# A hybrid diffusion block: the low part of each streamed weight block is subtracted on GpSimd instead of VectorE

## The chip, the cores and the metric

The kernel runs on one core of one Trainium2 chip. The metric is the device time of one execution in microseconds (us), lower is better. Times given here are the median of several executions; the profile is one execution, and its times count from its first instruction.

The core has five engines that run side by side and wait for each other by semaphores: TensorE (PE in the rows; its weight loads are PEld), VectorE (DVE), ScalarE (ACT), GpSimd (POOL) and SyncE (SP), which issues most of the transfers. Each engine takes its own instructions in order. SBUF is the on-chip memory, PSUM the memory that TensorE writes.

## The reference

Two layers. Each normalises and modulates 512 latent and 256 context tokens of width 1024, and projects them by `w_in` to the inputs of four branches and of four gates. The mixing part is the sum over the branches (a Fourier mix, a convolution, grouped attention, differential attention) of gate times projected branch, and one output projection; a gated feed-forward part follows.

```python
px = jnp.split(hx @ w_in[l], SPLIT_IDX, axis=-1)
...
gates = jax.nn.sigmoid(zgate.reshape(b, l, N_BRANCH, D_MODEL))
ys = jnp.stack([y_four, y_conv, y_gqa, y_diff], axis=2)
return jnp.sum(gates * ys, axis=2) @ lp["w_out"]
```

All is float32. The second layer leaves out the context's own output.

## The kernel before, in words

**Products in three.** Activations lie with features on the 128 partitions and tokens along the row. Each float32 operand of a large product is split into a high part, rounded to the matmul type `float32r`, and a low part, the rest; a product is three matmuls: high by high, high by low, low by high (`mm3u`, lines 603 to 605: weight high `wh` with activations high, with activations low, then weight low `wl` with activations high).

**Streamed weight blocks.** A weight block is 512 rows by 128 columns, in SBUF a 128x512 tile of 256 KB. In the mixing part from the key and query projections on, 264 blocks come through the class `Stream`. Each takes three steps: `dma` issues the load of `ws` on SP (line 553), `hi` rounds it to `wh` on ScalarE (line 559), `lo` subtracts `wl = ws - wh` on VectorE (line 566). There are three buffers of `ws` and four each of `wh` and `wl`. `feed` is called after every six matmuls of a unit; it does at most one `lo`, then at most one `hi` (only while fewer than four `wh` are held), then loads as far as there are `ws` buffers. So a `lo` stands one feed after its `hi`, and a block is made while the unit before it is multiplied. The other weight loads (`wload`, `wsplit`, lines 212 to 226: convolution and Fourier inputs, `w_out`, feed-forward) have their own subtraction on VectorE (line 216), with the same buffers.

**Units and stretches.** A unit is one column block of a projection: two weight blocks for a query, key or value projection, three for a gate (two of `w_in`, one of the branch's output weights). The tokens go in two halves in layer 0 (384 columns) and in one piece of 512 columns in layer 1, so a gate unit of layer 0 is 72 matmuls, 36 to a half. The mixing part has two kinds of stretch. In the attention stretches (grouped, then differential) a `Filler` puts pieces of units between the steps of the softmax (`scores` line 900, `row_max` 906 to 910, `exps` 919, `transp` 929 to 932, values by weights 1339 or 1428, evacuation 1347 to 1351 or 1438 to 1439). In the dense stretch (`dense`, line 1473) units follow each other, and in layer 0 VectorE beside them works out the next modulation vectors from `w_ada` (`ada_steps`, lines 130 and 132, then a matmul with ones, line 140).

**What sets the order.** In the attention stretches the order of TensorE, VectorE and ScalarE is the order in which the program is written (`manual_schedule`, line 1247). Elsewhere, and on GpSimd and SP everywhere, a scheduler orders the instructions by a timeline that it works out while building.

**What else VectorE and GpSimd do there.** VectorE runs the taps of the convolution (line 697, one `scalar_tensor_tensor` each: `ca += w * ub`), rotary positions (795 to 799), splits of queries (816) and keys (828), all of them with two tiles of SBUF as inputs, and the softmax's own steps, most of them with one input in PSUM (932, 1350, 1351). GpSimd raises small statistics to a power (line 165: `r`, `rq`), spreads the reciprocals of the softmax's sums over 128 columns (line 1284: `sb`), and issues a few transfers (824, 829: copies of split keys `khl`; 1242, 1258, 1016).

Of the kernel before, what the change touches and what calls it, by code (L numbers as in the profile page):

```python
# [62 lines left out]
def block_kernel(ctx: ExitStack, tc: tile.TileContext, x, c, ctx_in, c_ctx, w_ada, b_ada, norm_mix, w_in,  # L63
# [3 lines left out]
    nc = tc.nc  # L67
# [100 lines left out]
    def affine(h, k, lo, hi, v, mod, oA, oB, on_act):  # L168
        for a, b, rr in segs(lo, hi):
            sc, sh = mod[:, oA + k, rr:rr + 1], mod[:, oB + k, rr:rr + 1]  # L170
            o = v[:, a - lo:b - lo]
            if on_act:
                nc.scalar.activation(o, o, AF.Identity, scale=sc, bias=sh)
            else:
                nc.vector.tensor_scalar(o, o, sc, sh, op0=ALU.mult, op1=ALU.add)
        nc.scalar.copy(h[:, 0, k, lo:hi], v)  # L176
        lastn[0] = nc.vector.tensor_sub(h[:, 1, k, lo:hi], v, h[:, 0, k, lo:hi]).ins  # L177

    def norm_range(bank, xs, h, mod, oA, oB, lo, hi):
        nt = (hi - lo) // P  # L180
        acc = ttile(hi - lo, "nacc")
        for k in range(NC_):
            if k == 0:
                nc.scalar.activation(acc, xs[k][:, lo:hi], AF.Square)
            else:
                sq = ttile(hi - lo, "nsq")
                nc.scalar.activation(sq, xs[k][:, lo:hi], AF.Square)
                nc.vector.tensor_add(acc, acc, sq)
        yield
        pst = bank()  # L190
        for t in range(nt):
            nc.tensor.matmul(pst[:, t:t + 1], lhsT=acc[:, t * P:(t + 1) * P], rhs=ones2[:, 0:1], start=True, stop=True)
        r = rstd(pst[:, :nt], nt, 1.0 / D, EPS)
        yield
        pb = bank()
        for t in range(nt):
            nc.tensor.transpose(pb[:, t * P:(t + 1) * P], r[:, t:t + 1].to_broadcast([P, P]), ident)
        with tc.manual_schedule(engines=AD):
            hns = []
            for k in range(NC_ + 1):  # L200
                if k < NC_:
                    hn = ttile(hi - lo, "hn")
                    nc.vector.tensor_mul(hn, xs[k][:, lo:hi], pb[:, :hi - lo])
                    hns.append(hn)
                if k:
                    affine(h, k - 1, lo, hi, hns[k - 1], mod, oA, oB, True)
# [340 lines left out]
    class Stream:  # L547
# [15 lines left out]
        def lo(self, u):  # L563
            i = len(u.wt)
            wl = wp.tile([P, 4, P], F32R, tag="wl", name="wl")
            nc.vector.tensor_sub(wl, u.raw[i], u.wh[i])  # L566
            u.wt.append([(u.wh[i][:, k], wl[:, k]) for k in range(4)])
            self.raw -= 1

# [45 lines left out]
    for l in range(DEPTH):  # L615
# [10 lines left out]
        with ExitStack() if l else first as st:  # L626
# [24 lines left out]
            def utile(n, name):  # L651
                return sp.tile([P, NU], F32, tag="u", name=name, bufs=5)[:, :n]
# [58 lines left out]
            for cch in range(4):  # L711
                u = utile(NU, "ub")
# [991 lines left out]
```

## Time and profile before

| What | Value |
|---|---|
| median of 3 runs | 2656.47 us (2656.05 to 2658.01) |
| span of the profiled execution, first to last instruction | 2653.6 us |
| median of the runs less the profiled span | 2.87 us |
| TensorE matmuls, busy | 2575.0 us, 97% of the span |
| VectorE busy | 1690.8 us, 64% |
| ScalarE busy | 1129.0 us, 43% |
| GpSimd busy | 113.1 us, 4% |
| the subtraction of line 566 on VectorE | 264 times, 181.1 us in all |

Busy time is the time in which an engine had an instruction at work. TensorE's matmuls overlap, so that one of 384 columns shows as some 0.34 us while the next starts some 0.17 us later. "Idle before, releaser" is the time an engine stood still ahead of an instruction and what ended that wait. Rows of the timeline give start, duration, engine, line, operation, tiles, shape and count, and in brackets the idle time ahead with its releaser.

### The profile page before, as it was taken

Reading aid. Unit: us, or ns where it says so; the run is one execution under the profiler, and the core shown is the slowest. Engines: PE = TensorE matmul, PEld = TensorE weight load, DVE = VectorE, ACT = ScalarE, POOL = GpSimd, SP = SyncE. Lnnn points to the kernel's source line nnn. Section 1 sums busy time; section 2 is a strip of 40 time slices with the busy share of each in tenths; the row PEclk is TensorE's granted clock in tenths of the full one; section 3 lists DMA queues with packets and bytes.
Section 4 is the critical chain, followed back from the end, with each engine's and each line's share of the span. In section 5 each row is a group of like instructions: output and inputs, shape, how many; then the busy total and the mean of one; then the engine's idle time right before and its main releaser. Section 6 shows DMA issues by size and latency. Waiting matters only on the chain.

```text
span 2653.6 us, 38963 instructions
## 1 busy us (share of the span) xinstructions
PE 2575.0 (97%) x14779; PEld 2363.2 (89%) x14779; DVE 1690.8 (64%) x3010; ACT 1129.0 (43%) x2262; POOL 113.1 (4%) x179
## 2 busy tenths in 40 slices
PE   7999999999999999999999999999999999999998
PEld 5999889999999988999999988778888888888887
DVE  5967887786878467553443479987766535733335
ACT  5245555556421245212212254565655424633235
POOL 2000000010000000000000000000000000000000
PEclk9999999999999999999999999999999999999999
DMA  8211112222245255342443453111222234533334
GB/s 290 68 41 44 44 33 72 60 58 70 82 146 172 82 163 155 102 132 77 121 129 96 129 147 92 49 43 50 67 80 68 76 96 146 156 102 97 93 98 136
DMA packets 401759, 263.07 MB, mean 99 GB/s; under 512 B 15882, under 2 KB 369492, under 8 KB 401572
## 3 DMA queue, kind: packets, MB, share of 16 engines
q1 hardware_dynamic: 394292, 236.67, 30.2%
q0 software_dynamic: 7280, 23.93, 3.2%
q8 instruction: 116, 1.90, 0.3%
q14 instruction: 71, 0.58, 0.1%
HBM read 243.75 MB, written 8.91 MB: 95 GB/s over the span
## 4 chain that ended last, share of the span: by engine, by line
PE 84%; DVE 5%; ACT 4%; issue 3%; DMA 3%; POOL 0%; DVEq 0%; POOLq 0%; SPq 0%; ACTq 0%
PE pf L521 14%; PE pf L519 14%; PE pf L520 14%; PE pf L603 10%; PE pf L604 10%; PE pf L605 10%; PE pS L900 3%; PE pT L929 2%; PE pv L1339 2%; PE pv L1428 1%; DMA ws<-in_w_ffn_dram 1%; ACT e L919 1%; DVE wl L216 1%; ACT wh L214 1%; DMA ws<-in_w_out_dram 1%
## 5 line engine op out<-in xcount | busy, mean ns | idle before, releaser
L214 ACT CAST wh<-ws 128x512 fp32r<-128x512 f32 (+1 forms) x432 | 261.7, 608 | 584.7 <-PE pf L520 437.5
L519 PE MATMUL pf<-h,wh 128*128 128x384 f32 (+2 forms) x1360 | 468.6, 347 | 6.0 <-ACT h L176 2.1
L520 PE MATMUL pf<-h,wh 128*128 128x384 f32 (+2 forms) x1360 | 468.5, 346 | 1.0 <-DVE h L177 1.0
L521 PE MATMUL pf<-h,wl 128*128 128x384 f32 (+2 forms) x1360 | 467.9, 346 | 0.5 <-DVE wl L216 0.4
L216 DVE TENSOR_TENSOR wl<-ws,wh 128x512 fp32r<-128x512 f32 (+1 forms) x432 | 289.6, 674 | 271.2 <-ACT wh L214 265.7
L603 PE MATMUL pf<-h,wh 128*128 128x384 f32 (+1 forms) x1280 | 459.5, 359 | 1.9 <-ACT tg L775 1.3
L605 PE MATMUL pf<-h,wl 128*128 128x384 f32 (+1 forms) x1280 | 449.1, 351 | 0.0
L604 PE MATMUL pf<-h,wh 128*128 128x384 f32 (+1 forms) x1280 | 448.2, 350 | 0.0
L519 PEld LDWEIGHTS pf<-h,wh 128*128 128x128 f32 x1360 | 254.9, 188 | 27.5 <-ACT h L176 3.8
L520 PEld LDWEIGHTS pf<-h,wh 128*128 128x128 f32 x1360 | 255.9, 188 | 20.4 <-DVE h L177 2.4
L521 PEld LDWEIGHTS pf<-h,wl 128*128 128x128 f32 x1360 | 255.5, 188 | 20.2 <-DVE wl L216 1.6
L559 ACT CAST wh<-ws 128x512 fp32r<-128x512 f32 x264 | 164.1, 623 | 238.2 <-PE pf L604 201.9
L603 PEld LDWEIGHTS pf<-h,wh 128*128 128x128 f32 x1280 | 241.9, 189 | 16.3 <-ACT tg L775 2.0
L604 PEld LDWEIGHTS pf<-h,wh 128*128 128x128 f32 x1280 | 242.0, 189 | 13.5 <-issue 0.6
L605 PEld LDWEIGHTS pf<-h,wl 128*128 128x128 f32 x1280 | 241.2, 188 | 13.4 <-issue 0.2
L566 DVE TENSOR_TENSOR wl<-ws,wh 128x512 fp32r<-128x512 f32 x264 | 181.1, 687 | 103.4 <-ACT wh L559 102.2
L697 DVE SCALAR_TENSOR_TENSOR ca<-ub,cols,ca 128x798 f32<-128x798 f32 (+1 forms) x240 | 215.3, 897 | 3.9
L130 DVE SCALAR_TENSOR_TENSOR wada<-wada,sil 128x512 f32<-128x512 f32 x224 | 162.1, 747 | 64.7 <-DMA wada<-in_w_ada_dram 63.9
L521 PE MATMUL pf<-g,wl 128*128 128x384 f32 (+2 forms) x584 | 198.7, 341 | 1.2 <-DVE wl L216 0.9
L519 PE MATMUL pf<-g,wh 128*128 128x384 f32 (+2 forms) x584 | 198.4, 341 | 0.6 <-ACT wh L214 0.6
L520 PE MATMUL pf<-g,wh 128*128 128x384 f32 (+2 forms) x584 | 197.6, 339 | 0.0
L931 ACT CAST pt<-pT 128x512 fp32r<-128x512 f32 (+1 forms) x216 | 91.9, 471 | 153.5 <-PE pT L929 153.0
(323 smaller groups left out, 4063.8 us busy)
## 6 DMA issues: line engine op xcount, KB each, us to landing
ws<-in_w_ffn_dram SPq DMA_DIRECT2D x284, 256.0 KB, 2.9
ws<-in_w_in_dram SPq DMA_DIRECT2D x248, 256.0 KB, 3.0
wada<-in_w_ada_dram SPq DMA_DIRECT2D x160, 256.0 KB, 2.9
ws<-in_w_out_dram SPq DMA_DIRECT2D x58, 256.0 KB, 3.0
ws<-in_w_ffn_dram SPq DMA_DIRECT2D x48, 192.0 KB
wada<-in_w_ada_dram SPq DMA_DIRECT2D x16, 512.0 KB, 6.8
khl<-khl POOLq DMA_DIRECT2D x40, 192.0 KB, 3.2
ws<-in_w_four_dram SPq DMA_DIRECT2D x16, 256.0 KB, 2.9
```

The costliest lines, as they stand in the source:

```text
L130: nc.vector.scalar_tensor_tensor(accs[r], w, s, accs[r], op0=ALU.mult, op1=ALU.add)
L214: nc.scalar.copy(wh[:, :n], st[:, :n])
L216: lastv[0] = nc.vector.tensor_sub(wl[:, :n], st[:, :n], wh[:, :n]).ins
L519: nc.tensor.matmul(o, lhsT=wh, rhs=xh(k), start=(k == 0), stop=False)
L520: nc.tensor.matmul(o, lhsT=wh, rhs=xl(k), start=False, stop=False)
L521: nc.tensor.matmul(o, lhsT=wl, rhs=xh(k), start=False, stop=(k == n - 1))
L559: nc.scalar.copy(wh, u.raw[len(u.wh)])
L566: nc.vector.tensor_sub(wl, u.raw[i], u.wh[i])
L603: nc.tensor.matmul(o, lhsT=wh, rhs=xh(k), start=(k == 0), stop=False)
L604: nc.tensor.matmul(o, lhsT=wh, rhs=xl(k), start=False, stop=False)
L605: nc.tensor.matmul(o, lhsT=wl, rhs=xh(k), start=False, stop=(k == nk - 1))
L697: nc.vector.scalar_tensor_tensor(a, u, w, a, op0=ALU.mult, op1=ALU.add)
```

## The change

The subtraction of line 566 is issued on GpSimd instead of VectorE. Nothing else is written differently.

```diff
         def lo(self, u):
             i = len(u.wt)
             wl = wp.tile([P, 4, P], F32R, tag="wl", name="wl")
-            nc.vector.tensor_sub(wl, u.raw[i], u.wh[i])
+            nc.gpsimd.tensor_sub(wl, u.raw[i], u.wh[i])
             u.wt.append([(u.wh[i][:, k], wl[:, k]) for k in range(4)])
             self.raw -= 1
```

VectorE in the grouped attention of layer 0, at the last token blocks of a head, before the change (`qhl` are split queries, `ca` a convolution sum, `yg` and `ss` the output and the sums of the softmax, `pt` its transposed weights):

```order
279 L816 TENSOR_TENSOR qhl<-qe,qhl 64x768 x2
280 L697 SCALAR_TENSOR_TENSOR ca<-ub,cols,ca 128x798 x2
281 L566 TENSOR_TENSOR wl<-ws,wh 128x512
282 L1350 TENSOR_TENSOR yg<-yg,pv 64x128 x2
283 L1351 TENSOR_TENSOR yg<-yg,pv 128x128
284 L1282 RECIPROCAL ss<-ss 128x2
```

The same place on VectorE with the change:

```order
251 L816 TENSOR_TENSOR qhl<-qe,qhl 64x768 x2
252 L697 SCALAR_TENSOR_TENSOR ca<-ub,cols,ca 128x798 x2
253 L1350 TENSOR_TENSOR yg<-yg,pv 64x128 x2
254 L1351 TENSOR_TENSOR yg<-yg,pv 128x128
255 L1282 RECIPROCAL ss<-ss 128x2
```

The subtraction is gone from between the taps and the evacuation; what stands around it keeps its order.

GpSimd at the start of the grouped attention of layer 0, the change against before (`rq` is a query norm's power, `sb` the spread reciprocals):

```order
 L1284 COPY sb<-ss 128x128
+L566 TENSOR_TENSOR wl<-ws,wh 128x512 x2
 L165 TENSOR_TENSOR rq<-var,mhalf 128x12
-L1284 COPY sb<-ss 128x128 x5
+L1284 COPY sb<-ss 128x128
+L566 TENSOR_TENSOR wl<-ws,wh 128x512
+L1284 COPY sb<-ss 128x128
+L566 TENSOR_TENSOR wl<-ws,wh 128x512 x2
```

The subtractions now stand one to three at a time between the copies and powers that GpSimd had to itself.

TensorE in the dense stretch of layer 0 before the change, where the first column sums of the modulation (line 140) are taken between a gate product (`h`) and a branch product (`yc`):

```order
3068 L603 MATMUL pf<-h,wh 128x384
3069 L604 MATMUL pf<-h,wh 128x384
3070 L605 MATMUL pf<-h,wl 128x384
3071 L140 MATMUL pS<-ones_80,wada 128x1
3072 L603 MATMUL pf<-yc,wh 128x384
```

The same with the change:

```order
3044 L604 MATMUL pf<-yc,wh 128x384
3045 L605 MATMUL pf<-yc,wl 128x384
3046 L1230 MATMUL pT<-ident,r 128x128 x3
3047 L140 MATMUL pS<-ones_80,wada 128x1 x4
3048 L603 MATMUL pf<-h,wh 128x384
```

The sums stand 24 matmuls earlier, ahead of the gate product instead of behind it. Other than this stretch and a few matmuls ahead of the grouped attention, TensorE's order is as before.

## Rows read from the trace of the kernel before

**Rows 1.** The page, busy time of the engines over the span, with shares and instruction counts.

```profile
PE 2575.0 (97%) x14779; PEld 2363.2 (89%) x14779; DVE 1690.8 (64%) x3010; ACT 1129.0 (43%) x2262; POOL 113.1 (4%) x179
```

**Rows 2.** Windows: stretch, its length, busy time of PE, PEld, DVE, ACT, POOL (with instruction counts), granted clock as a share of full speed, DMA share, GB/s. In order: grouped attention of layer 0, differential attention of layer 0, dense stretch of layer 0 (up to 870), grouped and differential attention of layer 1.

```profile
205.00:455.00 250.00, 237.24 (x1489) 226.83 (x1488) 196.56 (x357) 143.63 (x326) 19.91 (x37) 0.98 0.17 49
455.00:710.00 255.00, 249.87 (x1561) 243.38 (x1560) 187.32 (x341) 140.61 (x302) 15.04 (x22) 1.00 0.22 58
710.00:870.00 160.00, 159.39 (x963) 159.02 (x962) 133.22 (x225) 36.33 (x68) 3.54 (x4) 1.00 0.55 165
...
1695.00:1935.00 240.00, 226.82 (x1299) 197.11 (x1298) 192.20 (x347) 154.52 (x316) 15.54 (x28) 0.99 0.21 57
1935.00:2100.00 165.00, 159.99 (x883) 139.94 (x882) 110.54 (x183) 86.66 (x172) 9.47 (x12) 1.00 0.25 69
```

**Rows 3.** The timeline of PE: the first matmul after eight of its waits in the mixing part, with the idle time ahead and its releaser in brackets.

```profile
265.22 0.35 PE L1339 MATMUL pv<-pt,vg 128*128 128x256 f32 x1 [1.43 <-DVE ss L1282]
375.65 0.36 PE L1339 MATMUL pv<-pt,vg 128*128 128x256 f32 x1 [1.42 <-DVE ss L1282]
570.41 0.24 PE L966 MATMUL pT<-ones,vs 128*128 128x1 f32 x1 [0.51 <-DVE vs L959]
589.94 0.32 PE L973 MATMUL pT<-ident,r 128*128 128x128 f32 x1 [1.56 <-POOL r L165]
1708.20 0.33 PE L929 MATMUL pT<-ident,e 128*128 128x128 f32 x1 [0.34 <-DVE pt L932]
1735.40 0.33 PE L929 MATMUL pT<-ident,e 128*128 128x128 f32 x1 [1.28 <-DVE pt L932]
1775.49 0.33 PE L929 MATMUL pT<-ident,e 128*128 128x128 f32 x1 [1.88 <-DVE pt L932]
1912.55 0.32 PE L973 MATMUL pT<-ident,r 128*128 128x128 f32 x1 [0.54 <-POOL r L165]
```

**Rows 4.** The timeline of DVE: the subtraction of line 566 that ran ahead of each of these waits, in the same order (two at 587.35).

```profile
263.58 0.69 DVE L566 TENSOR_TENSOR wl<-ws,wh 128x512 fp32r<-128x512 f32 x1
374.01 0.69 DVE L566 TENSOR_TENSOR wl<-ws,wh 128x512 fp32r<-128x512 f32 x1
565.00 0.69 DVE L566 TENSOR_TENSOR wl<-ws,wh 128x512 fp32r<-128x512 f32 x1
587.35 1.29 DVE L566 TENSOR_TENSOR wl<-ws,wh 128x512 fp32r<-128x512 f32 x2
1705.80 0.69 DVE L566 TENSOR_TENSOR wl<-ws,wh 128x512 fp32r<-128x512 f32 x1 [0.82 <-ACT wh L559]
1733.19 0.69 DVE L566 TENSOR_TENSOR wl<-ws,wh 128x512 fp32r<-128x512 f32 x1
1773.29 0.69 DVE L566 TENSOR_TENSOR wl<-ws,wh 128x512 fp32r<-128x512 f32 x1
1910.61 0.68 DVE L566 TENSOR_TENSOR wl<-ws,wh 128x512 fp32r<-128x512 f32 x1
```

**Rows 5.** The timeline of DVE, then of ACT, around the first of these places.

```profile
259.56 1.94 DVE L816 TENSOR_TENSOR qhl<-qe,qhl 64x768 fp32r<-64x768 f32 x2 [1.39 <-ACT qhl L812]
261.53 2.14 DVE L697 SCALAR_TENSOR_TENSOR ca<-ub,cols,ca 128x798 f32<-128x798 f32 x2
...
264.19 0.57 DVE L1350 TENSOR_TENSOR yg<-yg,pv 64x128 f32<-64x128 f32 x2
264.79 0.29 DVE L1351 TENSOR_TENSOR yg<-yg,pv 128x128 f32<-128x128 f32 x1
...
260.41 0.62 ACT L559 CAST wh<-ws 128x512 fp32r<-128x512 f32 x1
...
262.26 0.62 ACT L559 CAST wh<-ws 128x512 fp32r<-128x512 f32 x1
```

**Rows 6.** All instructions of line 566: duration as least, median and largest in ns, first and last start, and what ended DVE's idle time before them (us, times). Under "who waited for it" the view has no row.

```profile
L566 DVE TENSOR_TENSOR wl<-ws,wh x264: 669/686/694, 132.5 to 2203.7; 128x512 fp32r<-128x512 f32 x132
...
  ACT wh L559: 102.2, 75
```

**Rows 7.** Groups of POOL by form: line, operation, tiles, shape, count, then busy us and mean ns of one, and idle before with releasers.

```profile
L165 POOL TENSOR_TENSOR rq<-var,mhalf 128x12 f32<-128x12 f32 x4 | 9.5, 2384 | 42.4 <-DVE var L163 42.4
...
L165 POOL TENSOR_TENSOR rq<-var,mhalf 128x8 f32<-128x8 f32 x4 | 7.4, 1862 | 26.0 <-DVE var L163 26.0
...
L324 POOL TENSOR_TENSOR mod<-mod,cols 128x4 f32<-128x4 f32 x2 | 0.4, 199 | 21.5 <-DVE mod L320 21.5
```

**Rows 8.** All copies of line 1284 on POOL (least, median, largest ns); then the timeline of POOL and of DVE around one of the long ones, and one beside a DVE instruction that reads PSUM.

```profile
L1284 POOL COPY sb<-ss x40: 279/294/585, 215.0 to 1846.6; 128x128 f32<-128x128 f32 x40
...
336.13 0.58 POOL L1284 COPY sb<-ss 128x128 f32<-128x128 f32 x1 [8.20 <-PE pT L929]
...
335.89 0.67 DVE L566 TENSOR_TENSOR wl<-ws,wh 128x512 fp32r<-128x512 f32 x1
...
303.18 0.29 POOL L1284 COPY sb<-ss 128x128 f32<-128x128 f32 x1 [7.08 <-DVE ss L1282]
...
303.30 0.69 DVE L932 TENSOR_TENSOR pt<-pT,pt 128x512 fp32r<-128x512 f32 x1 [0.28 <-ACT pt L931]
```

**Rows 9.** Groups of DVE in the dense stretch of layer 0 (710 to 870).

```profile
L130 DVE SCALAR_TENSOR_TENSOR wada<-wada,sil 128x512 f32<-128x512 f32 x109 | 78.3, 746 | 2.9 <-DMA wada<-in_w_ada_dram 2.3
L566 DVE TENSOR_TENSOR wl<-ws,wh 128x512 fp32r<-128x512 f32 x34 | 23.3, 684 | 5.8 <-ACT wh L559 5.8
```

## The prediction

> **What bounds the kernel now.** I read the page's busy times first. TensorE is busy for 97% of the span [rows 1], so what the change can give back is at most TensorE's idle time in the mixing part. The table by stretches comes next: length less busy time of PE is 12.8, 5.1, 0.6, 13.2 and 5.0 us in the grouped, differential and dense stretch of layer 0 and the two attention stretches of layer 1 [rows 2], 36.7 us together. VectorE is busy for 79%, 73%, 83%, 80% and 67% of them, so it is nowhere the bound on average; in the dense stretch TensorE hardly waits at all, and a lighter VectorE is worth nothing there. What counts is the single moments at which TensorE waits for the end of a queue on VectorE. So the third view is TensorE's waits one by one, each held against what VectorE did just before.
>
> **What is removed, and what that is worth.** VectorE loses 264 subtractions of 0.686 us, 181 us of busy time, and the 102.2 us for which it stood still behind `wh` with other work queued [rows 6]. Nearly all of that lies beside TensorE's work. On the path it counts only where an unbroken run of VectorE work with a subtraction in it ends in a wait of TensorE. I found eight such waits [rows 3, 4]. In the first, VectorE runs two query splits, two taps, the subtraction at 263.58 and then at 264.19 the evacuation that frees the PSUM tile TensorE waits for [rows 5]: the subtraction takes 264.19 - 263.58 = 0.61 us of the queue, of a wait of 1.43. Each wait is credited with 0.61 us, or with its whole length where that is less, and the fourth with twice that, 1.21, for its two subtractions:
>
> 0.61 + 0.61 + 0.51 + 1.21 + 0.34 + 0.61 + 0.61 + 0.54 = 5.04 us.
>
> What is late next is the same evacuation, still behind the splits and the taps; the waits get shorter and do not vanish. TensorE's other waits in these stretches end on ScalarE, on a transfer, or on VectorE without a subtraction ahead, and I credit them with nothing.
>
> **What is added: the time of one subtraction on GpSimd.** The trace has no GpSimd instruction of this shape. From below: a product of four columns from two inputs took 0.199 us [rows 7] and a copy of 128 columns from one input 0.294 [rows 8], so 0.095 us for 124 columns and one input, and 0.199 + 508 x 0.095 / 124 = 0.59 us. From above: four copies of 128 columns, for each of two inputs, 8 x 0.294 = 2.35 us. The powers do not serve as a bound: 2.4 us for 12 columns [rows 7] is the power and not the reading. I take 1.2 us, near four copies. In all that is 317 us of a GpSimd busy for 113 us in the whole span [rows 1]: throughput is no question. The Trainium skill ("GPSIMD Engine Reference", Performance versus the Vector engine) has an add of 2048 float32 columns at 4497 ns; a quarter of that is an estimate of 1.12 us, and by it the sum would be the same.
>
> **Is it in time?** Now no instruction on any engine waits for line 566 last [rows 6]. The margin follows from the four buffers. In the dense stretch of layer 0 a gate unit's second block can be rounded once a third of the previous unit's second half is done, and is first read when a third of the new unit's first half is done, 36 matmuls later; at 159.39 / 963 = 0.166 us each [rows 2] that is 6.0 us, less 0.62 for the rounding [rows 5]: 5.3 us for the subtraction. At 1.2 us, or at 2.35 behind a tap of 1.07 (half of the pair in [rows 5]) and a copy, it is in time. Only behind a power (2.4 us) as well is it about a us late, and there are eight powers `rq` [rows 7] between the subtractions. Behind the subtractions on GpSimd now stand the `sb` copies, the powers and the issue of the `khl` transfers; each can come later by one or two subtractions. A later subtraction also frees its `ws` later, but loads are limited by `wh` before that. These I put at 0 to 2 us, and take 0.5.
>
> **What GpSimd and VectorE do to each other.** This decides the sign. Of 40 copies of `sb`, the longest took 0.585 us against a median of 0.294 [rows 8]. The one at 336.13 began while VectorE was in a subtraction with two SBUF inputs (335.89 to 336.56) and ended 0.15 us after it; the one at 303.18 ran beside an instruction that reads PSUM, in 0.29 us [rows 8]. So here VectorE with two SBUF inputs holds GpSimd up. No row shows the other direction, VectorE held up by GpSimd, since nothing on GpSimd reads SBUF for long. Its price has two ends: nothing, or a whole subtraction of 1.2 us each time a two-input instruction of VectorE has to start meanwhile. And it falls on the places of the credit: in the first, `wh` blocks are ready at 261.03 and 262.88 (starts and durations of ScalarE in rows 5), in the middle of two splits and two taps, all with two SBUF inputs. If GpSimd gets in between them, the queue grows by 1.2 us, or by 2.4 with both blocks, where it was to shrink by 0.61.
>
> The value I take lies between: at half the places GpSimd gets its turn only when VectorE turns to PSUM, at the others it gets in once. That keeps half of the credit, 2.5 us; the other half is not only lost but costs 1.2 - 0.61 = 0.59 at the two back-to-back places among them, 1.2 us in all. With 0.5 us for the later GpSimd work: -2.5 + 1.2 + 0.5 = -0.8 us.
>
> The profiled execution spans 2653.6 us and the median of the runs is 2656.47; the 2.87 between them I carry over as they are. Changes of span are added to the median: 2656.47 - 0.8 = 2655.7 us. About 0.2%, 5.3 us, is what a measurement of this kernel can tell from no change.
>
> **The rivals.**
>
> *VectorE is never held up.* Then the whole credit comes in, and 0.5 is paid: 2656.5 - 5.0 + 0.5 = 2652 us, and if the shorter queues also reach waits of TensorE that end on ScalarE, for which I allow 2.5 us more, 2649.5. For it speaks that VectorE starts each instruction a little before the last one ends (264.19 against 263.58 + 0.69 [rows 4, 5]), which leaves no gap in a run; against it, that nothing shows which engine goes first.
>
> *VectorE is held up for the whole of each subtraction.* The place is the runs of two-input work. In attention the credit of 5.0 is gone, and at the four places where splits and taps run back to back (the first two and 1735.40 and 1775.49) one or two subtractions get in: 4 x (1.2 - 0.61) = 2.4 up to 4 x (2.4 - 0.61) = 7.2 us. In the dense stretch of layer 0 VectorE has 133.2 - 23.3 = 110 us of other work, 78 of it the modulation's two-input instructions [rows 2, 9]; 34 subtractions at 1.2 us raise it to 151 of 160 us. There the built order has TensorE take the column sums 24 matmuls earlier (4 us) than before, so that TensorE, which does not wait now, could wait for a late VectorE: 0 to 4 us. Together +2.4 to +11 us; I take +7: 2663.5 us. It decides from the point where GpSimd takes its turn between two VectorE instructions that follow each other without a gap. The Trainium skill ("SBUF — State Buffer", Who interferes with whom) speaks for it: a VectorE instruction with two SBUF inputs and a GpSimd instruction that reads SBUF exclude each other, and whichever starts first blocks the other fully. The copies above agree for the one direction; no run here shows the other.
>
> *GpSimd is late.* If a subtraction takes 2.35 us or more and stands behind powers, copies and unready inputs, TensorE waits for `wl`, which it never does now. Eight powers with a us each, less half of the credit: 8 - 2.5 = +5.5 us, 2662 us, and more if the subtraction is longer still. Against it stands the margin of 5.3 us.
>
> That the change doesn't do what it says is excluded by the built order: the subtractions stand on GpSimd, and VectorE's rows around them are unchanged.
>
> **How the numbers follow.** Between the ends, 0.48; never held up, 0.21; held up in full, 0.25; GpSimd late, 0.06. The likeliest is the first, with a range of its own of 2652 to 2660. The range for all reaches to 2649.5 on one side and to 2666.5 on the other, which leaves out a part of the two outer rivals. Faster by over 0.2% is below 2651.2: some half of the second case and a little of the first, 0.18. Slower by over 0.2% is above 2661.8: most of the third and the fourth case, 0.26. The rest, 0.56, is within 0.2%.
>
> **What would show it.** Line 566 appears on POOL 264 times with a median near 1.2 us, and a largest value some 1 us above it where it meets two-input VectorE work. VectorE's busy time falls by about 181 us if an instruction that is held up shows no longer duration; if taps, splits and the modulation's instructions have a larger mean than now, or gaps between them that nothing released, VectorE is held up, and the third case is at work. The waits of TensorE at the eight places shrink by 0.61 us each, or grow. In the dense stretch, waits at line 140 or behind line 782 would show the third case there; a row of TensorE waiting for `wl` of line 566 would show the fourth. The prediction is wrong if TensorE's idle time in the five stretches, 36.7 us now, changes by more than 5 us, or if time moves in stretches that have no streamed block.

## The result and the profile after

The changed kernel takes 2691.64 us, median of four runs (2689.52 to 2701.93), beside 2656.26 for the kernel before (2655.65 to 2658.01): a ratio of 1.0141, interval 1.0123 to 1.0159. It is slower by 1.4%, 35 us. The forecast was 2655.7 with a range up to 2666.5.

The profiled execution spans 2687.7 us, 34.1 more than before. From the page of the changed kernel, the busy time of the engines and three of its costliest groups:

```profile
PE 2590.1 (96%) x14779; PEld 2373.8 (88%) x14779; DVE 1630.5 (61%) x2746; ACT 1130.3 (42%) x2262; POOL 479.9 (18%) x443
...
L566 POOL TENSOR_TENSOR wl<-ws,wh 128x512 fp32r<-128x512 f32 x264 | 369.5, 1401 | 803.1 <-ACT wh L559 797.6
...
L697 DVE SCALAR_TENSOR_TENSOR ca<-ub,cols,ca 128x798 f32<-128x798 f32 (+1 forms) x240 | 241.6, 1006 | 4.8
L130 DVE SCALAR_TENSOR_TENSOR wada<-wada,sil 128x512 f32<-128x512 f32 x224 | 180.1, 832 | 82.8 <-DMA wada<-in_w_ada_dram 81.9
```

Against [rows 1] TensorE is busy for 15.1 us more with the same 14779 instructions, and idle for 19.0 us more: two losses, slower matmuls and longer waits. VectorE is without 264 instructions, but its busy time falls by 60 us only. Line 130 stood at 746 ns before [rows 9].

The changed kernel's groups of VectorE by form (busy us and mean ns in the middle) show which instructions got longer:

```profile
L697 DVE SCALAR_TENSOR_TENSOR ca<-ub,cols,ca 128x798 f32<-128x798 f32 x120 | 139.8, 1165 | 2.3
L906 DVE TENSOR_REDUCE nm<-pS 128x2 f32<-128x1536 f32 x64 | 112.2, 1754 | 10.4 <-PE pS L900 10.4
L697 DVE SCALAR_TENSOR_TENSOR ca<-ub,cols,ca 128x512 f32<-128x512 f32 x120 | 101.7, 848 | 2.5
L932 DVE TENSOR_TENSOR pt<-pT,pt 128x512 fp32r<-128x512 f32 x96 | 66.0, 687 | 76.3 <-ACT pt L931 76.0
...
L783 DVE TENSOR_TENSOR macc<-macc,tg 128x512 f32<-128x512 f32 x24 | 28.8, 1202 | 0.7
L1350 DVE TENSOR_TENSOR yg<-yg,pv 64x128 f32<-64x128 f32 x80 | 22.4, 280 | 30.3 <-ACT yg L1347 29.8
```

In the kernel before the two forms of line 697 take 1046 and 748 ns and that of line 783 takes 686. All three have two tiles of SBUF as inputs. Lines 906, 932 and 1350, which read PSUM (alone, or beside one tile of SBUF), keep their durations. Here and below an instruction is called held when it stands still because of one on the other engine. The single instructions say how long a hold lasts (least, median, largest ns, of the changed kernel; then line 908 of the kernel before):

```profile
L566 POOL TENSOR_TENSOR wl<-ws,wh x264: 1260/1295/2514, 134.9 to 2238.4; 128x512 fp32r<-128x512 f32 x132
...
L130 DVE SCALAR_TENSOR_TENSOR wada<-wada,sil x224: 734/750/1837, 726.4 to 1548.9; 128x512 f32<-128x512 f32 x112
...
L908 DVE TENSOR_SCALAR nm<-nm x40: 168/169/1133, 463.0 to 2108.9; 128x2 f32<-128x2 f32 x40
```
```profile
L908 DVE TENSOR_SCALAR nm<-nm x40: 160/169/171, 456.0 to 2074.9; 128x2 f32<-128x2 f32 x40
```

A subtraction takes 1.295 us on GpSimd. Line 130 goes from 0.75 up to 1.84, and line 908, two columns wide and with a single SBUF input, from 0.169 up to 1.133: an instruction of VectorE stands still for up to most of a subtraction. GpSimd is held in turn, up to 2.51 us.

The timeline of the changed kernel at the place of the first of [rows 3], on DVE, POOL and PE, and PE's row for the second:

```profile
264.68 1.94 DVE L816 TENSOR_TENSOR qhl<-qe,qhl 64x768 fp32r<-64x768 f32 x2 [1.40 <-ACT qhl L812]
266.65 3.93 DVE L697 SCALAR_TENSOR_TENSOR ca<-ub,cols,ca 128x798 f32<-128x798 f32 x2
...
266.22 1.54 POOL L566 TENSOR_TENSOR wl<-ws,wh 128x512 fp32r<-128x512 f32 x1 [4.81 <-ACT wh L559]
268.08 1.65 POOL L566 TENSOR_TENSOR wl<-ws,wh 128x512 fp32r<-128x512 f32 x1 [0.32 <-ACT wh L559]
...
271.54 0.47 PE L1339 MATMUL pv<-pt,vg 128*128 128x256 f32 x2 [2.63 <-DVE ss L1282]
381.63 0.47 PE L1339 MATMUL pv<-pt,vg 128*128 128x256 f32 x2 [2.62 <-DVE ss L1282]
```

The two taps took 2.14 us before [rows 5] and now take 3.93: 1.79 longer, with the two subtractions beside them. VectorE is rid of 0.61 us of subtraction there, and TensorE's wait grows by 1.79 - 0.61 = 1.18; the trace has 2.63 against 1.43.

The largest loss is in the dense stretch of layer 0. Windows of TensorE there (stretch, length, busy time of PE, granted clock, DMA share, GB/s): the whole stretch by the marks of the table below, in the changed kernel and then before, and four pieces of the changed kernel around one wait; then, from PE's timeline, the matmul behind that wait:

```profile
727.80:954.50 226.70, 219.69 (x1260) 0.97 0.43 129
716.30:926.80 210.50, 210.50 (x1259) 1.00 0.46 138
...
764.00:766.00 2.00, 1.40 (x10) 0.92 0.69 220
766.00:768.00 2.00, 2.00 (x8) 0.50 0.30 71
768.00:770.00 2.00, 2.00 (x10) 0.73 0.89 282
770.00:772.00 2.00, 2.00 (x13) 1.00 0.14 41
```
```profile
764.60 1.05 PE L140 MATMUL pS<-ones,wada 128*128 128x1 f32 x8 [1.35 <-DVE wada L130]
```

Before, TensorE was not idle in this stretch at all, at full clock (the 0.6 us of [rows 2] lie ahead of 716.3); now it is idle for 7.0 us, and at a mean clock of 0.97 it loses another 0.03 x 226.7 = 6.8 us, together 13.8 of the 16.1 us by which the stretch got longer. Behind the wait of 1.35 us the granted clock falls to 0.50, the lower of its two levels (1.2 of 2.4 GHz), while TensorE works without a gap. The three windows lose (0.08 + 0.50 + 0.27) x 2 = 1.7 us of full clock, which is 3.4 us at the lower level. Over the whole span the clock is 0.989 against 0.994: (1 - 0.989) x 2687.7 - (1 - 0.994) x 2653.6 = 13.6 us of full clock more are lost, as much as eight such falls, and about the 15.1 us by which the same matmuls are busy longer.

TensorE's waits in the changed kernel (us in all, times, longest), the five for VectorE that are new or have grown most; then the rows of the kernel before for waits of which this text speaks; and last a wait of ScalarE in the changed kernel:

```profile
PE pS L140 <- DVE wada L130: 6.7, 5, 2.6
...
PE pv L1339 <- DVE ss L1282: 6.1, 3, 2.6
...
PE pT L857 <- DVE ke L874: 3.6, 2, 1.8
PE pT L966 <- DVE vs L959: 3.5, 2, 2.6
...
PE pT L1062 <- DVE vg L1045: 2.7, 2, 1.7
```
```profile
PE pT L887 <- ACT vf L882: 5.6, 4, 1.9
...
PE pT L929 <- DVE pt L932: 3.8, 4, 1.9
PE pv L1339 <- DVE ss L1282: 3.7, 3, 1.4
...
PE pT L973 <- POOL r L165: 2.1, 2, 1.6
...
PE pT L1062 <- DVE vg L1045: 1.0, 1, 1.0
...
PE pT L966 <- DVE vs L959: 1.0, 2, 0.5
```
```profile
ACT wh L559 <- POOL wl L566: 37.4, 24, 3.3
```

The first and the third of the change have no row in the kernel before. The five grow by 6.7 + 2.4 + 3.6 + 2.5 + 1.7 = 16.9 us, of the 19.0 that TensorE is idle longer. No row has TensorE waiting for `wl` from GpSimd. ScalarE's rounding does wait for it, 24 times, but TensorE's waits that end on ScalarE are not longer for it: 29.2 us in all, 30.8 before.

Where the time went, by the starts of matmuls that end each stage (first of line 603, first of 900, last of 1339, of 1428, of 605 in either layer), one profiled execution each, us; the other columns are differences from before:

| Stage | before | change | zeros | attention only | elsewhere only | reads twice |
|---|---|---|---|---|---|---|
| start, to the first streamed product | 142.1 | +2.5 | +1.7 | +0.2 | +1.2 | +0.5 |
| layer 0, ahead of attention | 65.7 | +3.9 | 0.0 | 0.0 | +5.5 | +3.9 |
| layer 0, grouped | 232.3 | +1.7 | -5.4 | +0.9 | -1.8 | +4.0 |
| layer 0, differential | 276.2 | +3.5 | -4.5 | +3.1 | +0.4 | +12.2 |
| layer 0, dense | 210.6 | +16.1 | 0.0 | 0.0 | +16.6 | +6.9 |
| feed-forward and on | 712.3 | -0.5 | +0.8 | +0.2 | -0.3 | +1.2 |
| layer 1, ahead of attention | 56.1 | +6.8 | +0.3 | +1.7 | +6.1 | +8.2 |
| layer 1, grouped | 168.8 | +0.7 | -6.0 | +1.9 | -2.9 | +1.4 |
| layer 1, differential | 224.7 | 0.0 | -2.7 | -0.1 | +0.1 | +8.2 |
| layer 1, dense | 125.2 | 0.0 | 0.0 | 0.0 | 0.0 | 0.0 |
| to the end | 439.7 | -0.5 | -1.3 | 0.0 | +1.5 | +2.9 |

Stages without streamed blocks differ by up to 3 us among these executions (the start and the end), which is how far a single mark can be read; one fall of the clock alone is 1.7 us. The last four columns are the first four experiments.

### The profile page after: what moved, and what is told of

Same layout as the page of the kernel before. It is cut to its first block, busy times and chain, and to the rows that moved or that the text cites. A ratio compares the mean times of both kernels' runs of the same rounds, so it can differ in the third digit from the quotient of the medians.

```text
span 2687.7 us, 39054 instructions
## 1 busy us (share of the span) xinstructions
PE 2590.1 (96%) x14779; PEld 2373.8 (88%) x14779; DVE 1630.5 (61%) x2746; ACT 1130.3 (42%) x2262; POOL 479.9 (18%) x443
## 5 line engine op out<-in xcount | busy, mean ns | idle before, releaser
L566 POOL TENSOR_TENSOR wl<-ws,wh 128x512 fp32r<-128x512 f32 x264 | 369.5, 1401 | 803.1 <-ACT wh L559 797.6
L605 PEld LDWEIGHTS pf<-h,wl 128*128 128x128 f32 x1280 | 244.0, 191 | 13.5 <-issue 0.2
L697 DVE SCALAR_TENSOR_TENSOR ca<-ub,cols,ca 128x798 f32<-128x798 f32 (+1 forms) x240 | 241.6, 1006 | 4.8
L130 DVE SCALAR_TENSOR_TENSOR wada<-wada,sil 128x512 f32<-128x512 f32 x224 | 180.1, 832 | 82.8 <-DMA wada<-in_w_ada_dram 81.9
L932 DVE TENSOR_TENSOR pt<-pT,pt 128x512 fp32r<-128x512 f32 (+1 forms) x216 | 107.7, 535 | 96.3 <-ACT pt L931 95.8
```

The source lines that it names most:

```text
L130: nc.vector.scalar_tensor_tensor(accs[r], w, s, accs[r], op0=ALU.mult, op1=ALU.add)
L566: nc.gpsimd.tensor_sub(wl, u.raw[i], u.wh[i])
L605: nc.tensor.matmul(o, lhsT=wl, rhs=xh(k), start=False, stop=(k == nk - 1))
L697: nc.vector.scalar_tensor_tensor(a, u, w, a, op0=ALU.mult, op1=ALU.add)
```

## The experiments

The theory after the result: a subtraction on GpSimd and an instruction of VectorE that reads SBUF twice exclude each other, for as long as the first runs. Rivals: the other order on TensorE that the scheduler made from the change; blocks that come late; a shared bandwidth instead of an exclusion. Edits are shown against the kernel before, unless said otherwise.

**The change in the attention stretches only, and its complement.** A flag `pool` of the class `Stream` is set from line 1248 to line 1461, or outside of it.

```diff
-            nc.vector.tensor_sub(wl, u.raw[i], u.wh[i])
+            (nc.gpsimd if self.pool else nc.vector).tensor_sub(wl, u.raw[i], u.wh[i])
```

> The subtraction is on GpSimd only in the attention stretches, whose order is written out by hand; in the other stretches it is on VectorE, and TensorE's order in the dense stretch is that of before. Theory of the port (VectorE instructions with two SBUF inputs stand still for a whole GpSimd subtraction): only the attention's share of the loss, some 5 to 9 us, 2661 to 2665, with taps (line 697) up to 1.2 us longer and the waits of TensorE at lines 1339 and 929 longer by as much. Theory of the order (the scheduler puts TensorE's column sums and head statistics where VectorE cannot yet have delivered): no loss, 2651 to 2657. Theory of late blocks (TensorE is held up by low parts that come later): waits on wl in attention, some 10 us.

> The complement: GpSimd subtracts only outside the hand-ordered attention, that is ahead of the grouped attention and in the dense stretches; TensorE's order is that of the change throughout. Port: 4 + 16 + 7 us of the traces' difference stay, 2681 to 2686, and with the first run of this set the two losses add up to about 35. Order: the whole loss stays, 2688 to 2693. Late blocks: most of the loss, with waits on wl.

In attention only: 2664.78 us, ratio 1.0038 (1.0023 to 1.0053). Elsewhere only: 2685.68, ratio 1.0113 (1.0098 to 1.0128). Some 10 and 30 us, 40 together against the 35 of the change: the loss is roughly the sum of its places, and three quarters of it lie ahead of attention and in the dense stretch, where the credit had no place. In attention the hold takes back all of the relief and more: by the marks the four stretches are 5.8 us longer, where VectorE has 150 subtractions less.

**No reading on GpSimd.** GpSimd fills `wl` with zeros, twice, so the low part of the streamed weights is left out of the result; TensorE does all its matmuls.

```diff
-            nc.vector.tensor_sub(wl, u.raw[i], u.wh[i])
+            nc.gpsimd.memset(wl.bitcast(F32), 0.0); nc.gpsimd.memset(wl.bitcast(F32), 0.0)
```

> GpSimd fills wl with zeros twice instead of subtracting: the low part of the streamed weights is left out, so GpSimd writes as much SBUF or more and reads none, and TensorE's order in the dense stretch is that of the change. Port (it is the reading that excludes): 2650 to 2656, no VectorE group longer than before. Order: the dense stretch and the stretch ahead of the attention keep their loss, 2675 to 2685. If writing excludes as well: as slow as the change.

2641.39 us, ratio 0.9953 (0.9937 to 0.9970). The page of this run (busy times and the group of line 697), and TensorE's waits:

```profile
PE 2570.3 (97%) x14779; PEld 2360.5 (90%) x14779; DVE 1534.0 (58%) x2746; ACT 1128.5 (43%) x2262; POOL 385.8 (15%) x707
...
L697 DVE SCALAR_TENSOR_TENSOR ca<-ub,cols,ca 128x798 f32<-128x798 f32 (+1 forms) x240 | 215.4, 898 | 4.8
```
```profile
PE pT L887 <- ACT vf L882: 3.3, 4, 1.2
PE pv L1339 <- DVE ss L1282: 2.5, 3, 0.8
...
PE pT L929 <- DVE pt L932: 1.5, 2, 1.3
...
PE pT L973 <- POOL r L165: 0.7, 2, 0.5
...
PE pT L966 <- DVE vs L959: 0.5, 1, 0.5
```

GpSimd writes the same tiles, 528 fills with a median of 0.526 us, 278 us in all, and VectorE's instructions keep their durations (line 697: 897 ns over both forms before, 898 here). So what the change promised was there: 14 us, more than was expected of this run, and all of it in the attention stretches (18.6 us by the marks of the profiled execution). And the hold costs 2691.6 - 2641.4 = 50 us. VectorE's busy time without the subtraction is 1534.0, so that of the change is longer by 96 us through holds. (The 121 us in the expectation for the halves below was worked out by taking 181 off the page of before, which is too much, since neighbouring instructions overlap a little.) The order is that of the change but for a few instructions (38 of 14779 on TensorE, 4 of 2746 on VectorE), and the dense stretch and those ahead of attention cost nothing more: by itself the order is harmless.

**Reading on GpSimd without relief.** VectorE subtracts as before, and GpSimd subtracts once more, into the raw block that is then dead.

```diff
-            nc.vector.tensor_sub(wl, u.raw[i], u.wh[i])
+            nc.vector.tensor_sub(wl, u.raw[i], u.wh[i]); nc.gpsimd.tensor_sub(u.raw[i], u.raw[i], u.wh[i])
```

> VectorE subtracts as before, and GpSimd subtracts once more, into the raw tile that nobody needs any longer; the result is unused. TensorE's order in the dense stretch is that of before. Port: VectorE keeps its own 181 us and is held up besides, so at least the loss of the change, 2690 to 2720. Order: nearly nothing, 2655 to 2660.

2701.04 us, ratio 1.0176 (1.0161 to 1.0191). The groups of line 697 and line 566 on VectorE:

```profile
L566 DVE TENSOR_TENSOR wl<-ws,wh 128x512 fp32r<-128x512 f32 x264 | 193.4, 734 | 87.0 <-ACT wh L559 85.8 <-issue 0.3
...
L697 DVE SCALAR_TENSOR_TENSOR ca<-ub,cols,ca 128x798 f32<-128x798 f32 x120 | 134.0, 1117 | 1.9
...
L697 DVE SCALAR_TENSOR_TENSOR ca<-ub,cols,ca 128x512 f32<-128x512 f32 x120 | 98.8, 824 | 2.0
```

The results of this subtraction are never used, so no low part can be late. The raw block comes free later, but TensorE has no wait for `wh` or `wl` of a streamed block in this trace. The time is lost all the same: 46 us. That this is near the 50 above is in part chance, because it is lost in other places: 20 us in the two differential stretches, where the change loses 3.5, and some of it behind GpSimd's own powers (line 973 behind `r`: 6.5 us, 2.1 before). In the dense stretch TensorE's order is that of before; the same holds (line 130 has a mean of 910 ns in that stretch here, 917 in the change) cost 6.9 us instead of 16. So the earlier column sums of the change do matter, but only together with a VectorE that is held.

**The subtraction in two halves, and fills beside the subtraction.**

```diff
-            nc.vector.tensor_sub(wl, u.raw[i], u.wh[i])
+            for q in (0, 2): nc.gpsimd.tensor_sub(wl[:, q:q + 2], u.raw[i][:, q:q + 2], u.wh[i][:, q:q + 2])
```
```diff
-            nc.vector.tensor_sub(wl, u.raw[i], u.wh[i])
+            nc.vector.tensor_sub(wl, u.raw[i], u.wh[i]); nc.gpsimd.memset(u.raw[i], 0.0); nc.gpsimd.memset(u.raw[i], 1.0)
```

> The change, with each GpSimd subtraction made by two instructions of 256 columns instead of one of 512; nothing is left out. Theory 1 (a GpSimd instruction that reads SBUF keeps a VectorE instruction with SBUF inputs waiting until the GpSimd instruction ends): the wait has the length of one GpSimd instruction, so halves of about 0.7 us each cut the longest instructions: the maxima of line 130 and line 783 fall from 1.8 to about 1.4 us or less. VectorE gets in between the two halves, so the sum of its lengthening falls from 121 us to between 60 and 110 us, and the time from 2691 to 2670 to 2685 us. Theory 2 (both engines share a bandwidth and each instruction runs slower in proportion to the overlap): the maxima and the lengthening stay as in the change, and the two instructions' fixed cost (2 x about 0.7 us against 1.3 us) leaves the time at 2690 to 2697 us.

> The kernel before with two GpSimd fills of 128x512 behind each VectorE subtraction, into the raw block that is then dead; nothing is left out. GpSimd is busy for 264 x 2 x 0.52 = 272 us and only writes. Theory 1 (reading excludes, not writing): VectorE's rows keep the durations of the kernel before (line 697 1046 and 748 ns, line 130 747 ns), and the time is 2653 to 2659 us. Rival (any work of GpSimd in SBUF holds VectorE, and the run with zeros hid it behind the relief of VectorE): line 130 above 770 ns, line 697 above 1070 ns, the time above 2665 us. A third way, that the raw block comes free later (by about 1 us, so its next DMA starts 1 us later) and TensorE waits for blocks: waits of TensorE for wl or wh in the rows, 2660 us or more.

Halves: 2677.08 us, ratio 1.0078 (1.0065 to 1.0092). Fills: 2657.77, ratio 1.0009 (1.0000 to 1.0018). The busy times of the halves' page, then all their instructions of line 566 and of line 130 (least, median, largest ns):

```profile
PE 2589.6 (97%) x14779; PEld 2371.9 (89%) x14779; DVE 1600.9 (60%) x2746; ACT 1129.8 (42%) x2262; POOL 562.7 (21%) x707
```
```profile
L566 POOL TENSOR_TENSOR wl<-ws,wh x528: 712/740/1957, 132.8 to 2221.8; 128x256 fp32r<-128x256 f32 x176
...
L130 DVE SCALAR_TENSOR_TENSOR wada<-wada,sil x224: 732/750/1277, 716.3 to 1537.9; 128x512 f32<-128x512 f32 x112
```

GpSimd is busy for 83 us more than in the change, and the kernel is 14.6 us faster: the longest hold follows the length of one GpSimd instruction (line 130 up to 1.28 instead of 1.84 us), and VectorE is held for 1600.9 - 1534.0 = 67 us instead of 96. A shared bandwidth would have made it no better. In the dense stretch of layer 0 the waits at line 140 fall from 6.7 to 4.3 us, and yet the stretch keeps 14.3 of its 16.1 us: its mean clock is 0.97 here as well, so shorter waits brought the clock down just as much. Beside 277 us of fills, line 697 keeps 1047 and 748 ns, and the time stays.

**Beside an instruction that reads PSUM.** The row maximum of line 906 takes 1.75 us and kept its duration in every run. So here a subtraction goes to GpSimd only there: VectorE copies one column into `wl` just ahead of the row maximum, which starts GpSimd through the tile. If nothing is put off, 14 subtractions are open at that moment; to have more, the grouped and differential stretches put a subtraction off while at least one, two or three finished blocks are in hand.

```diff
-        def lo(self, u):
+        def lo(self, u, S=None):
...
-            nc.vector.tensor_sub(wl, u.raw[i], u.wh[i])
+            S is None or nc.vector.tensor_copy(wl[:, 0, 0:1], S[:, 0, 0:1]); (nc.vector if S is None else nc.gpsimd).tensor_sub(wl, u.raw[i], u.wh[i])
...
-                    self.lo(u)
+                    if not self.pool or self.held - self.freed - sum(len(v.wh) - len(v.wt) for v in units) < 3: self.lo(u)
...
-                nc.vector.reduce_max(nm, S[:, :, :nk], axis=AX.X, negate=True)
+                next((stream.lo(u, S) for u in fill.g[:3] + fill.nx[:3] if nk == NTOK and len(u.wh) > len(u.wt)), None); nc.vector.reduce_max(nm, S[:, :, :nk], axis=AX.X, negate=True)
```

> The kernel before, in which only 64 of the 264 subtractions go to GpSimd, each started by VectorE (through a copy of one column into its wl tile, about 0.1 us) just ahead of the row maximum of line 906, which takes 1.75 us and reads PSUM alone; in grouped and differential attention the other subtractions are put off while at least one finished block is in hand; nothing is left out. Theory 1: the 1.3 us on GpSimd lie beside an instruction that isn't held, so line 697 and line 1378 keep their durations of before (1046 and 748 ns, 1019 ns), and VectorE loses 64 x (0.67 - 0.1) = 36 us in attention; the run with zeros took 14 us off the time with 150 subtractions gone there, so this takes about 64/150 x 18 = 6 us: 2645 to 2652 us. If a block finished late makes TensorE wait (one in hand is little), 2655 to 2665 us. Rival (VectorE is held whatever stands beside it): line 697 above 1080 ns, the time 2658 to 2665 us.

> As the last, with at least two finished blocks in hand before a subtraction is put off (63 of 264 go to GpSimd). Theory 1: rows of line 697 and 1378 as in the kernel before and 2645 to 2652 us, with no TensorE wait for wl. Rival (VectorE is held all the same): line 697 above 1080 ns, 2658 to 2665 us. If the one-column copy and the row maximum that it delays by about 0.1 us cost what the relief gives: 2654 to 2658 us.

With one block in hand 2767.88 us, ratio 1.0423 (1.0409 to 1.0437); with two 2667.34, ratio 1.0051 (1.0037 to 1.0064). With two in hand, all subtractions on GpSimd (least, median, largest ns), the group of line 697, and TensorE's waits for `wl`:

```profile
L566 POOL TENSOR_TENSOR wl<-ws,wh x63: 1261/1285/1298, 209.5 to 2073.6; 128x512 fp32r<-128x512 f32 x63
```
```profile
L697 DVE SCALAR_TENSOR_TENSOR ca<-ub,cols,ca 128x798 f32<-128x798 f32 x120 | 125.6, 1047 | 1.9
```
```profile
PE pf L605 <- DVE wl L566: 8.9, 6, 2.1
...
PE pf L605 <- POOL wl L566: 4.6, 3, 3.2
```

The theory of the hold stands: not one of 63 subtractions is longer than 1.298 us, where the change has 2.514, and no tap is longer. The forecast of the time missed, and with one block in hand even the clause for late blocks (2655 to 2665) fell far short: with so little in hand TensorE waits for `wl`, 13.5 us with two blocks, most of it in grouped attention of layer 0, which gets 14.7 us longer.

> The ride beside the row maximum with nothing put off: only the subtractions that are open anyway when a row maximum of 1.75 us is issued go to GpSimd (14 of 264); nothing is left out. TensorE's order is that of the kernel before. Theory 1: no VectorE row is longer than in the kernel before, no TensorE wait for wl as in the last run (13.5 us), and the relief is 14 x (0.69 - 0.16) = 7 us of VectorE, by the run with zeros about 14/150 x 18 = 2 us of time: 2652 to 2656 us. Rival (the start behind the row maximum itself makes blocks late): TensorE waits for wl from GpSimd in the rows, 2657 to 2662 us.

> As the run in which subtractions were put off with two finished blocks in hand, now with three: 34 of 264 go to GpSimd; nothing is left out. Theory: the 14.7 us lost there in grouped attention of layer 0 came from blocks finished late (13.5 us of TensorE waits for wl), and with one more block in hand these waits fall under 3 us; 34/150 x 18 = 4 us of relief: 2649 to 2655 us. Rival (the order of the VectorE work, not the stock of blocks, makes the waits): 2660 us or more, with the waits for wl still above 8 us.

> The put-off with two finished blocks in hand in layer 1 alone; in layer 0 nothing is put off (37 of 264 go to GpSimd in all); nothing is left out. TensorE's order is that of the kernel before. Theory: the 4.5 us won in grouped attention of layer 1 come back and the 14.7 us lost in layer 0 go: 2648 to 2653 us, grouped attention of layer 1 4 to 5 us shorter than before, no VectorE row lengthened. Rival (the gain there is given back where the stages meet): 2654 to 2657 us.

With nothing put off 2654.64 us, ratio 0.9998 (0.9989 to 1.0007): 14 subtractions are too few to show. With three blocks in hand 2648.17, ratio 0.9971 (0.9959 to 0.9982), a little below the forecast, and no wait for `wl`: the fastest of all kernels here that compute the whole reference, 43 us below the change with an eighth of its subtractions on GpSimd. With two in hand in layer 1 alone 2653.49, ratio 0.9991 (0.9982 to 1.0000): the grouped stretch there is 4.8 us shorter, as forecast, but the whole gain is not told from nothing with certainty.

The control: the same put-off with three blocks in hand, and VectorE makes these 34 subtractions itself at the same place.

```diff
-            S is None or nc.vector.tensor_copy(wl[:, 0, 0:1], S[:, 0, 0:1]); (nc.vector if S is None else nc.gpsimd).tensor_sub(wl, u.raw[i], u.wh[i])
+            nc.vector.tensor_sub(wl, u.raw[i], u.wh[i])
```

> As the run with three finished blocks in hand, in the same order on TensorE, but VectorE itself makes the 34 subtractions where that run had its one-column copies, ahead of the row maximum; GpSimd gets none, and nothing is left out. It tells the gain of that run (0.9971 of the kernel before) apart into putting the work off and giving it to GpSimd. Theory 1 (GpSimd's share is the gain): each of the 34 puts its row maximum 0.69 - 0.16 = 0.53 us later, so 2652 to 2662 us, 4 us or more above that run. Rival (putting the work off is the gain): 2646 to 2651 us, the same stages shorter.

2658.38 us, ratio 1.0009 (1.0000 to 1.0017). By whole times, GpSimd's share is all of the gain. By the marks of the two profiled executions it is less plain: the four attention stretches are 9.2 us shorter than before with GpSimd and 5.7 without, so putting the work off gives more than half of it, and 3.5 us, about what a single mark can be read to, are seen at the place. The rest of the difference lies in stages in which both kernels do the same, 3.8 us of it at the start, where the lower clock cost 6.8 us without GpSimd and 3.4 with it. In the median of all runs the granted clock is 0.993 without and 0.995 with, some 5 of the 10 us between the two kernels; why it differs in those stages is open.

## Why the prediction was wrong

**What bounds the kernel** was read rightly: all of the loss is TensorE idle or slowed behind VectorE, and the averages told nothing. TensorE's idle time in the five stretches, by the marks, goes from 36.7 to 49.1 us, beyond the 5 us that the prediction named as a sign of being wrong. But the sentence that a lighter VectorE is worth nothing in the dense stretch was taken for the whole story of that stretch; a VectorE that gets slower there costs 16 us.

**The credit of 5.04 us** came true where nothing takes it away. In the run with zeros the four kinds of wait it was counted at (lines 1339 behind `ss`, 929 behind `pt`, 966, 973) fall from 3.7 + 3.8 + 1.0 + 2.1 = 10.6 to 2.5 + 1.5 + 0.5 + 0.7 = 5.2 us. It was too small as the worth of the whole: waits that end on ScalarE shrank as well (line 887 behind `vf` 5.6 to 3.3 us), and matmuls were busy for 4.7 us less. With the 5.4 that is 12.4 of the 17.0 us between the two profiled spans (2653.6 and 2636.6).

**The subtraction on GpSimd**, taken at 1.2 us, takes 1.295, well inside its bounds. The estimate from the Trainium skill's figure, 1.12 us ("GPSIMD Engine Reference", Performance versus the Vector engine), is a seventh too low here; with it the prediction's own sum comes to -1.0, not quite the same. **In time** was right: TensorE never waits for `wl` of GpSimd in the change, so the rival of the late GpSimd falls. The 0.5 us for GpSimd's other work coming later is not seen either: TensorE's waits that end on GpSimd go from 2.1 to 1.5 us.

**What GpSimd and VectorE do to each other** is the step that failed: "at half the places GpSimd gets its turn only when VectorE turns to PSUM, at the others it gets in once", worth -0.8 us in all with the 0.5 for later work. GpSimd does get in between two VectorE instructions that follow each other without a gap, at the first place between the splits and the taps and again between the taps. Beside 264 subtractions of 1.295 us, 342 us, VectorE stood still for 96 us. The value was put in the middle between two ends without a row for it. The one row near it, the `sb` copy that took twice its median and ended 0.15 us after VectorE's instruction [rows 8], shows a hold in the other direction alone.

**The rival "VectorE is held up for the whole of each subtraction"** had the mechanism and its arithmetic: at the first two places it gave 1.2 less 0.61 with one subtraction in between, or 2.4 less 0.61 with two; two got in, and the trace has 1.79 - 0.61 = 1.18, between the two. The Trainium skill's rule ("SBUF — State Buffer", Who interferes with whom) that a VectorE instruction with two SBUF inputs and a GpSimd instruction reading SBUF exclude each other, and that one which only writes does not, agrees with these runs: 96 us of holds in the change, and no two-input instruction longer in the run with zeros or beside the fills. What was wrong with this rival was its size, +7 of at most +11 against +35, in three terms. It counted the hold at the places of the credit alone, and left out the stages ahead of attention, where no wait had earned a credit (3.9 and 6.8 us). It gave the dense stretch 0 to 4 us, by adding up VectorE's work against its length (151 of 160 us); TensorE there waits for single column sums, and the stretch got 16 us longer. And it had no price for the clock: behind waits such as the one of 1.35 us TensorE goes on for some us at the lower level, 13.6 us of full clock in all, more than a third of the loss.

## What to carry to other kernels

Before work is moved from VectorE to GpSimd, look at what VectorE will run beside it: if those instructions read SBUF twice, each can be held for the length of a GpSimd instruction, and where they meet the work has not left VectorE's queue but grown in it, here from 0.69 us to a hold of as much as 1.1 (line 130, 1.84 against 0.75), though of 0.36 on average over all 264. Such work is worth moving to moments at which VectorE reads PSUM for long enough, started from that moment. Cut in two where they were not so placed, the subtractions cost less (0.8% instead of 1.4), but still cost. Where TensorE is nearly always busy, price a new wait with the slower matmuls that the trace shows behind such waits.

## What the runs showed that I had not expected

VectorE instructions with one SBUF input are held as well, where they are `tensor_scalar` in float32: line 908, two columns wide, up to 1.133 us instead of 0.169. GpSimd's fills, which leave the two-input work alone, hold these too: beside them line 132 (512 columns) goes up to 0.830 us from a median of 0.480. The Trainium skill's section named above lists `tensor_scalar` among the forms that can take the ports shared with GpSimd; the trace agrees, even for two columns.

The granted clock falls while TensorE is working again, just after the wait (the windows from 764 to 770), so a wait can cost more than its length. PE's timeline there in the changed kernel (start, us, line), at the lower level and a little later:

```profile
766.48 0.53 PE L603 MATMUL pf<-h,wh 128*128 128x384 f32 x1
766.80 0.53 PE L604 MATMUL pf<-h,wh 128*128 128x384 f32 x1
...
770.49 0.33 PE L604 MATMUL pf<-h,wh 128*128 128x384 f32 x1
770.66 0.33 PE L605 MATMUL pf<-h,wl 128*128 128x384 f32 x1
```

One matmul starts 0.32 us behind the other, and 0.17 us at full clock.
